# Seven products in one PSUM bank and another order of the steps, in a two-layer decoder trunk on one core

## The chip, the cores and the metric

One core of a Trainium2 chip runs the whole kernel. The metric is the device time of one execution in microseconds. TensorE (PE) multiplies, VectorE (DVE) and ScalarE (ACT) do the element work, GpSimd (POOL) and SyncE (SP) here only issue DMAs.

## The reference

Two layers; each is `x + mixed @ w_out`, with one input projection that feeds four groups of four heads. Cut to what matters:

```python
h = rms_norm(x, norm_g)                       # x: 256 x 2048
p = split_columns(h @ w_in)                   # q, k, v, gate of each group, and small ones
fox  = forgetting_attention(q, k, v, log_sigmoid(fox_f + fox_fb))
diff = rms_norm(softmax(q1 k1) v - lam * softmax(q2 k2) v)
moba = causal attention (256 keys are one block)
gla  = gated linear attention, in chunks of 64
mixed = concat([fox, diff, moba, gla], each times silu(its gate))
x = x + mixed @ w_out
```

After the second layer one more RMS norm. All inputs and the output are float32.

## The kernel before

**Weights.** Each weight tile is split into a high part (`hi`, written by ACT) and the rest (`lo`, written by DVE as weight minus high part), and so is the activation (`hTp` for the projections, `mTh` and `mTl` for the mixed groups in the output projection). A product is the sum of three: activation high by weight high, activation low by weight high, activation high by weight low. The weights stream in the order of use: SP loads them in steps of 512 KB, that is two 128 x 512 tiles, into five buffers (`raw`); `hi` and `lo` have four buffers, and are made three steps ahead of PE. A **block** is 512 columns of the projection in eight steps; a normal step is 12 matmuls with 512 columns, for two row tiles of 128 rows (`m` is 0 and 1) in one PSUM bank each. At a block's end ACT or DVE read the two banks (the evacuation).

**The seven products.** diff's and MoBA's values (`diff_v`, `moba_v`) are not projected in blocks but together, by Strassen's scheme: seven products p1 to p7 of sums of the quarters, four **form steps** of 6 matmuls each, 28 per layer. The sums of weights come by accumulating DMAs on POOL, those of activations from DVE. A form step uses up one 512 KB load in half the PE time of a normal step. Two PSUM banks take turns for the products.

**PSUM.** Eight banks of 128 x 512 float32: four for blocks and products (`mm0a`, `mm0b`, `mm1a`, `mm1b`), two pairs for everything else (`side`).

**What sets the order.** The program is written out step by step in a loop: `prepare(i + 3)` issues the hi part of a later step, then PE's matmuls of step `i`, then `tick()` gives out side work, then `complete(i + 3)` issues the lo part. Every engine takes its instructions in that order. Side work (rotary, softmax, gates, GLA, the norms) consists of generator tasks. `tick` keeps a small model of time: `times.now` moves with PE's matmuls, every DVE and ACT operation has a modelled end, and a task gets its next turn when its data is modelled to be there within LEAD (1.5 us). No more side work is given out while DVE's or ACT's modelled queue (`v_.tail`, `a_.tail`) reaches more than AHEAD past now. The side matmuls of a task stand in PE's queue at the place where the task was given its turn, so if the model was too hopeful, PE stands still there.

**Data that has to be transposed** goes through `turned`: a DVE stream transpose, four DMA writes on SP to a buffer in DRAM (`far`), and one DMA on POOL that reads it back. The model counts 4.5 us for the write, 6.5 for the read. The names in the profile: `four` and `eight` are working tiles of the side tasks; `fz` is FoX's forget gate, `an` GLA's small input, `fe` the exponentials that lead to `fz`.

**A task's PSUM.** `take_side` and `take_both` wait for a free pair of side banks.

The lines: L436 is the helper that issues nearly every matmul, L270 the helper of DVE and ACT operations, L276 that of DMAs through `far`, L1395 and L1359 the weight loads.

Of the kernel before, what the change touches and what calls it, by code (L numbers as in the profile page):

```python
# [21 lines left out]
P = 128  # L22
# [4 lines left out]
H = 4  # L27
# [82 lines left out]
def _blocks():  # L110
# [10 lines left out]
    for l in range(DEPTH):  # L121
        for cols in (
# [24 lines left out]
def _pair_steps(l):  # L147
# [3 lines left out]
    if not BY_DMA:  # L151
        raws.update({"p6": ("22",), "p4": ("21",)})
    return [{"pair": l, "form": f, "c": c, "from": [(q, c) for q in raws.get(f, ())], "first": c == 0, "last": c == 3}
            for f in ("p1", "p5", "p6", "p3", "p7", "p2", "p4") for c in range(4)]


NAMES = {13: "diff_v", 15: "moba_v"}


def _steps():  # L160
# [35 lines left out]
    for s in steps:  # L196
        if "pair" in s:
            s["at"] = {q: place((s["pair"], q), P * 1024) for q in s["from"] + [("12", s["c"])] * (s["form"] == "p1")}
# [5 lines left out]
def pair_part(q, c):  # L204
# [3 lines left out]
    return kts, COL[NAMES[PAIR[int(q[1]) - 1]]]  # L208
# [134 lines left out]
def hybrid_trunk(  # L343
# [52 lines left out]
    ranks = {"now": 0}  # L396
    ready = set()
    env = {}
    wakes = {}

    def tick(limited=True):
# [3 lines left out]
        for t in list(tasks):  # L405
            if max(v_.tail, a_.tail) > times.now + AHEAD:
                break
            for _ in range(3):
                if wakes[id(t)] > times.now + LEAD:
                    break  # L410
                times.latest, ranks["now"] = 0.0, ranks[id(t)]
                try:
                    next(t)
                except StopIteration:
                    tasks.remove(t)
                    del ranks[id(t)], wakes[id(t)]
# [1352 lines left out]
```

## Time and profile before

| | |
|---|---|
| median of 3 runs | 928.11 us (927.74 to 928.21) |
| the profiled execution's own time | 931.0 us |
| its span, first to last instruction | 928.9 us |
| mean granted TensorE clock | 0.986 |
| busy: PE, DVE, ACT | 893.5, 662.8, 563.7 us |
| data moved by DMA | 227.44 MB, 245 GB/s in the mean |

A row of the timeline or of a list of groups gives start and duration in us, engine, line, operation, output and inputs, and in square brackets how long the engine idled just before it and what ended that. A row of the waits gives what an engine waited for: us in all, how often, and the longest. Buffer numbers are left out of the profile's names.

### The profile page before, as it was taken

Reading aid. Unit: us, or ns where it says so; the run is one execution under the profiler, and the core shown is the slowest. Engines: PE = TensorE matmul, PEld = TensorE weight load, DVE = VectorE, ACT = ScalarE, POOL = GpSimd, SP = SyncE. Lnnn points to the kernel's source line nnn. Section 1 sums busy time; section 2 is a strip of 40 time slices with the busy share of each in tenths; the row PEclk is TensorE's granted clock in tenths of the full one; section 3 lists DMA queues with packets and bytes.
Section 4 is the critical chain, followed back from the end, with each engine's and each line's share of the span. In section 5 each row is a group of like instructions: output and inputs, shape, how many; then the busy total and the mean of one; then the engine's idle time right before and its main releaser. Section 6 shows DMA issues by size and latency. Waiting matters only on the chain.

```text
span 928.9 us, 12468 instructions
## 1 busy us (share of the span) xinstructions
PE 893.5 (96%) x4380; PEld 756.8 (81%) x4380; DVE 662.8 (71%) x943; ACT 563.7 (61%) x850; POOL 61.6 (7%) x87
## 2 busy tenths in 40 slices
PE   9989999999998999989999989999999989999996
PEld 7977789888786788878899868898878768788886
DVE  6679767688784884837668958777885849565783
ACT  6577665566654666735656965464863646575561
POOL 1001100001100000100000011000101000010100
PEclk9999999999998999999999999999999989999998
DMA  8769877648898477876878798676799763969952
GB/s 297 260 192 301 296 236 227 213 162 249 235 304 310 158 250 273 272 271 206 286 236 285 254 319 223 182 233 222 236 308 313 257 223 123 311 199 302 321 158 91
DMA packets 84141, 227.44 MB, mean 245 GB/s; under 512 B 9979, under 2 KB 30443, under 8 KB 83950
## 3 DMA queue, kind: packets, MB, share of 16 engines
q1 hardware_dynamic: 73336, 192.00, 60.6%
q0 software_dynamic: 9152, 33.03, 13.7%
q10 hardware_dynamic: 1590, 1.62, 0.6%
q8 instruction: 34, 0.56, 0.2%
q14 instruction: 29, 0.24, 0.1%
HBM read 204.06 MB, written 22.55 MB: 244 GB/s over the span
## 4 chain that ended last, share of the span: by engine, by line
PE 75%; DMA 11%; DVE 6%; issue 3%; ACT 3%; SPq 1%; POOL 0%; ACTq 0%; DVEq 0%; POOLq 0%
PE mm0a L436 16%; PE mm0b L436 15%; PE mm1b L436 15%; PE mm1a L436 15%; PE side L436 13%; DMA raw<-in_weights 6%; DMA far<-four 3%; DVE lo L270 3%; DMA four<-far 2%; DVE four L270 1%; ACT hi L270 1%; ACT four L270 1%; DMA four<-in_gla_wa 0%; DVE mx L270 0%; SPq L276 0%
## 5 line engine op out<-in xcount | busy, mean ns | idle before, releaser
L270 DVE TENSOR_TENSOR lo<-raw,hi 128x1024 fp32r<-128x1024 f32 (+2 forms) x319 | 363.6, 1156 | 126.8 <-ACT hi L270 118.9
L270 ACT ACTIVATE hi<-raw 128x1024 fp32r<-128x1024 f32 (+2 forms) x319 | 316.5, 1009 | 196.7 <-PE mm0b L436 52.1
L436 PE MATMUL mm0a<-hi,hTp 128*128 128x512 f32 (+1 forms) x448 | 168.3, 385 | 2.6 <-ACT hi L270 2.2
L436 PE MATMUL mm1a<-hi,hTp 128*128 128x512 f32 (+1 forms) x448 | 168.1, 384 | 2.4 <-ACT four L270 1.9
L436 PE MATMUL mm0b<-hi,hTp 128*128 128x512 f32 (+1 forms) x432 | 162.9, 382 | 0.1
L436 PE MATMUL mm1b<-hi,hTp 128*128 128x512 f32 (+1 forms) x432 | 162.6, 382 | 0.1
L436 PEld LDWEIGHTS mm0a<-hi,hTp 128*128 128x128 f32 x448 | 84.7, 189 | 19.7 <-ACT hi L270 3.8
L436 PEld LDWEIGHTS mm1a<-hi,hTp 128*128 128x128 f32 x448 | 84.6, 189 | 18.3 <-ACT four L270 2.3
L436 PEld LDWEIGHTS mm1b<-hi,hTp 128*128 128x128 f32 x432 | 81.7, 189 | 14.9 <-ACT four L270 0.8
L436 PEld LDWEIGHTS mm0b<-hi,hTp 128*128 128x128 f32 x432 | 81.9, 189 | 14.7 <-ACT four L270 0.6
L436 PE MATMUL mm0a<-lo,hTp 128*128 128x512 f32 (+1 forms) x224 | 84.3, 382 | 0.8 <-DVE lo L270 0.7
L436 PE MATMUL mm1a<-lo,hTp 128*128 128x512 f32 (+1 forms) x224 | 83.7, 380 | 0.4 <-DVE lo L270 0.4
L436 PE MATMUL mm0b<-lo,hTp 128*128 128x512 f32 (+1 forms) x216 | 81.2, 379 | 0.0
L436 PE MATMUL mm1b<-lo,hTp 128*128 128x512 f32 (+1 forms) x216 | 81.0, 379 | 0.0
L276 POOL DMA_DIRECT2D four<-far x40 | 22.1, 553 | 525.7 <-DMA far<-four 169.0
L436 PE MATMUL side<-four,four 128*128 128x128 f32 (+3 forms) x336 | 41.4, 302 | 12.1 <-DMA four<-far 6.6
L436 PEld LDWEIGHTS side<-four,four 128*128 128x128 f32 (+1 forms) x336 | 39.5, 208 | 15.7 <-DMA four<-far 7.4
L436 PEld LDWEIGHTS mm0a<-lo,hTp 128*128 128x128 f32 x224 | 42.4, 189 | 9.3 <-DVE lo L270 1.6
L436 PEld LDWEIGHTS mm1a<-lo,hTp 128*128 128x128 f32 x224 | 42.1, 188 | 8.3 <-DVE lo L270 0.8
L436 PEld LDWEIGHTS mm0b<-lo,hTp 128*128 128x128 f32 x216 | 40.8, 189 | 7.2
L436 PEld LDWEIGHTS mm1b<-lo,hTp 128*128 128x128 f32 x216 | 40.5, 188 | 7.2
L270 ACT ACTIVATE four<-four 128x512 fp32r<-128x512 f32 (+3 forms) x44 | 35.2, 821 | 17.1 <-DMA four<-far 14.1
(190 smaller groups left out, 1272.4 us busy)
## 6 DMA issues: line engine op xcount, KB each, us to landing
raw<-in_weights SPq DMA_DIRECT2D x271, 512.0 KB, 5.1
four<-far POOLq DMA_DIRECT2D x34, 512.0 KB, 6.4
far<-four SPq DMA_DIRECT2D x128, 128.0 KB, 4.9
raw<-in_weights SPq DMA_DIRECT2D x46, 348.0 KB, 4.4
xs<-in_weights POOLq DMA_DIRECT2D x24, 512.0 KB, 8.6
xs<-in_weights SPq DMA_DIRECT2D x8, 512.0 KB, 7.3
xs<-in_x SPq DMA_DIRECT2D x4, 512.0 KB, 10.4
kept<-xs SPq DMA_DIRECT2D x1, 2048.0 KB, 8.1
```

The costliest lines, as they stand in the source:

```text
L270: return f(*args, **kw)
L276: self.eng.dma_start(out, src, **kw)
L436: t_.matmul(out, lhsT, rhs, start=start, stop=stop, **kw)
```

## The change

- The form steps stand one by one: after steps 3, 6 and 8 of each block from the 3rd to the 11th, and one in the 12th. Before, two or three in a row stood behind each of these blocks.
- The order of the products is p2, p5, p3, p1, p6, p7, p4 where it was p1, p5, p6, p3, p7, p2, p4. diff's values are complete after 24 form steps (before 20), MoBA's after 28 (as before).
- All seven products use one PSUM bank. The other three banks of the four rotate among the blocks (`mm0` to `mm3`); before, the products held a pair and the blocks the other pair.
- In a block's first and last step the matmuls of row tile 0 all come ahead of those of row tile 1 (before they alternated), but for the first three steps of the program.
- The evacuation of a block is issued ahead of the next hi part, before behind it.
- The model: AHEAD 5.0 where it was 3.0; write 5.0 and readback 7.5 where they were 4.5 (3.0 in one place) and 6.5; a task that takes side banks waits until SAFE (1.0 us) past its data's modelled end, and times of data are handed from task to task (`given_out`, `until`).

The counts of instructions on PE, DVE, POOL and SP stay as they are; ACT has four table loads fewer. Two evacuations of products go from ACT to DVE and two from DVE to ACT.

```diff
@@ -37,19 +37,27 @@
...
-PAIR = (15, 13)
-FORMS_AFTER = {3: 3, 4: 3, 5: 3, 6: 2, 7: 3, 8: 3, 9: 3, 10: 3, 11: 3, 12: 2}
-WITHIN = {12: 2}
+MIDDLE = ("gla_v", "fox_q", "fox_k", "fox_v", "fox_g", "diff_q", "diff_k", "moba_q", "moba_k", "diff_g", "moba_g", "moba_v", "diff_v")
+NAMES = ("moba_v", "diff_v")
+PAIR = tuple(3 + MIDDLE.index(z) for z in NAMES)
+FORMS_AT = {i: (3, 6, 8) for i in range(3, 12)}
+FORMS_AT[12] = (3,)
+FORM_ORDER = ("p2", "p5", "p3", "p1", "p6", "p7", "p4")
...
-SUM_OF = {"p5": 3, "p6": 0, "p3": 1, "p7": 2}
+SUM_OF = {"p5": 3, "p3": 0, "p6": 1, "p7": 2}
...
-AHEAD = 3.0
+AHEAD = 5.0
...
+SAFE = 1.0
+ROOM = 5.0
+WRITE = 5.0
+READ = 7.5
@@ -151,10 +153,7 @@
...
-            for f in ("p1", "p5", "p6", "p3", "p7", "p2", "p4") for c in range(4)]
-NAMES = {13: "diff_v", 15: "moba_v"}
+            for f in FORM_ORDER for c in range(4)]
...
 def _steps():
@@ -175,14 +174,10 @@
...
-        for i, n in FORMS_AFTER.items():
+        for i, places in FORMS_AT.items():
...
-            within = WITHIN.get(i, 0)
-            if within:
-                at = own[len(own) // 2]
-                steps[at:at] = [rest.popleft() for _ in range(within)]
-            at = own[-1] + 1 + within
-            steps[at:at] = [rest.popleft() for _ in range(n - within)]
+            for z, at in enumerate(places):
+                steps.insert(own[0] + at + z, rest.popleft())
@@ -384,43 +379,50 @@
...
     def take_side():
+        yield SAFE
...
     def take_both():
+        yield SAFE
...
-    ranks = {"now": 0}
-    ready = set()
+    ranks = {"now": 0, "task": None, "room": AHEAD}
+    ready = {}
...
+    ends = {}
+    def given_out(key):
+        ready[key] = max(times.latest, ends.get(ranks["task"], 0.0))
...
     def tick(limited=True):
...
-            if max(v_.tail, a_.tail) > times.now + AHEAD:
+            if v_.tail > times.now + AHEAD or a_.tail > times.now + ranks["room"]:
...
-                times.latest, ranks["now"] = 0.0, ranks[id(t)]
+                times.latest, ranks["now"], ranks["task"] = 0.0, ranks[id(t)], id(t)
...
-                    next(t)
+                    more = next(t)
...
-                    del ranks[id(t)], wakes[id(t)]
+                    del ranks[id(t)], wakes[id(t)], ends[id(t)]
...
-                wakes[id(t)] = times.latest
-        ranks["now"] = 0
+                ends[id(t)] = max(ends[id(t)], times.latest)
+                wakes[id(t)] = ends[id(t)] + LEAD + more if more else times.latest
+        ranks["now"], ranks["task"], times.latest = 0, None, 0.0
...
     def begin(task, l, gi=None):
...
-        ranks[id(task)], wakes[id(task)] = rank, 0.0
+        ranks[id(task)], wakes[id(task)], ends[id(task)] = rank, times.latest, times.latest
@@ -428,6 +430,8 @@
     def until(key):
...
+        times.latest = max(times.latest, ready[key])
+        yield
...
     def matmul(out, lhsT, rhs, start, stop, tiles=1, **kw):
@@ -468,9 +472,9 @@
...
-            q_.move(d[:, :, i].rearrange("j c f -> c j f"), t[32 * i:32 * i + 32].rearrange("c (j f) -> c j f", j=4), 4.5)
-        yield
-        g_.move(t, d.rearrange("j c i f -> (j c) (i f)"), 6.5)
+            q_.move(d[:, :, i].rearrange("j c f -> c j f"), t[32 * i:32 * i + 32].rearrange("c (j f) -> c j f", j=4), WRITE)
+        yield
+        g_.move(t, d.rearrange("j c i f -> (j c) (i f)"), READ)
@@ -1555,33 +1561,30 @@
...
-        a, b = st["ps"]
-        for i, at in ((0, "p1"), (1, "p5")):
+        a = st["ps"]
+        for i, at in ((0, "p2"), (1, "p5")):
             if f == at:
...
-        r0 = r1 = env["r", l]
-        nr = env["r", l, -1.0]
-        if f == "p1":
-            a_.activation(st["t", 0][:, 0], a, AF.Copy, scale=r0[:, 0:1])
+        r, nr = env["r", l], env["r", l, -1.0]
+        left, right = st["t", 0], st.get(("t", 1))
+        if f == "p2":
+            a_.activation(left[:, 0], a, AF.Copy, scale=r[:, 0:1])
         elif f == "p5":
-            a_.activation(st["t", 1][:, 1], b, AF.Copy, scale=r1[:, 1:2])
+            a_.activation(right[:, 1], a, AF.Copy, scale=r[:, 1:2])
+        elif f == "p3":
+            a_.activation(right[:, 0], a, AF.Copy, scale=r[:, 0:1])
+        elif f == "p1":
+            v_.scalar_tensor_tensor(left[:, 0], a, r[:, 0:1], left[:, 0], op0=OP.mult, op1=OP.add)
         elif f == "p6":
-            a_.activation(st["t", 1][:, 0], a, AF.Copy, scale=nr[:, 0:1])
-        elif f == "p3":
-            t = st["t", 1][:, 0]
-            v_.scalar_tensor_tensor(t, b, r1[:, 0:1], t, op0=OP.mult, op1=OP.add)
+            v_.scalar_tensor_tensor(right[:, 0], a, nr[:, 0:1], right[:, 0], op0=OP.mult, op1=OP.add)
         elif f == "p7":
-            t = st["t", 1]
-            v_.scalar_tensor_tensor(t[:, 1], a, nr[:, 1:2], t[:, 1], op0=OP.mult, op1=OP.add)
-            given(l, PAIR[1], t)
-        elif f == "p2":
-            t = st["t", 0]
-            v_.scalar_tensor_tensor(t[:, 0], b, r0[:, 0:1], t[:, 0], op0=OP.mult, op1=OP.add)
+            v_.scalar_tensor_tensor(right[:, 1], a, nr[:, 1:2], right[:, 1], op0=OP.mult, op1=OP.add)
+            given(l, PAIR[1], right)
         elif f == "p4":
-            a_.activation(st["t", 0][:, 1], a, AF.Copy, scale=r0[:, 1:2])
-            given(l, PAIR[0], st["t", 0])
+            a_.activation(left[:, 1], a, AF.Copy, scale=r[:, 1:2])
+            given(l, PAIR[0], left)
...
     def given(l, i, t):
@@ -1610,10 +1613,12 @@
...
-        for x, part, j, kt in products:
-                for m in range(2):
-                    matmul(ps[m][:, :n], x[:, kt, m * P:(m + 1) * P], s[part][:, j],
-                           s["first"] and j == 0 and x is lh and part == "hi", part == "lo" and (True, j) == end)
+        products = [(*z, m) for z in products for m in range(2)]
+        if (s["first"] or s["last"]) and not any(s is z for z in plan[:HALVED]):
+            products.sort(key=lambda z: z[4])
+        for x, part, j, kt, m in products:
+            matmul(ps[m][:, :n], x[:, kt, m * P:(m + 1) * P], s[part][:, j],
+                   s["first"] and j == 0 and x is lh and part == "hi", part == "lo" and (True, j) == end)
...
     def results(b):
@@ -1648,26 +1653,30 @@
...
-    banks = {"n": 1, "s": None}
+    banks = {"next": deque(range(4)), "s": None}
...
     def settle(waiting, bank=None):
...
-                if bank is None or all(b["bank"] != bank for b in waiting):
+                if bank is None or all(bank not in b["banks"] for b in waiting):
...
+            times.latest = 0.0
...
-    def take_bank(k):
+    def take_bank(keep=True):
+        k = banks["next"].popleft()
+        if keep:
+            banks["next"].append(k)
...
-        return [mm.tile([P, 512], F32, name=f"mm{k}{m}", bufs=1) for m in "ab"]
+        return k, mm.tile([P, 512], F32, name=f"mm{k}", bufs=1)
@@ -1693,44 +1702,46 @@
...
+        if banks["s"] is not None and "done" in pairs[banks["s"]]:
+            banks["next"].append(pairs[banks["s"]]["bank"])
+            banks["s"] = None
+        settle(waiting)
         prepare(i + ahead)
...
-        if banks["s"] is not None and "done" in pairs[banks["s"]]:
-            banks["s"] = None
-        settle(waiting)
-        while not s["need"] <= ready:
+        while not s["need"] <= ready.keys():
...
-            if s["form"] == "p1" and s["first"]:
-                k = 1 - banks["n"]
-                pairs[s["pair"]] = {"bank": k, "ps": take_bank(k)}
+            if s["form"] == FORM_ORDER[0] and s["first"]:
+                k, ps = take_bank(False)
+                pairs[s["pair"]] = {"bank": k, "ps": ps}
...
-                ready.add(("paired", s["pair"], SUM_OF[s["form"]]))
+                given_out(("paired", s["pair"], SUM_OF[s["form"]]))
...
-                b["bank"] = None
+                b["banks"] = ()
...
-                    b["bank"] = banks["n"] = 1 - (banks["n"] if banks["s"] is None else pairs[banks["s"]]["bank"])
-                    b["ps"] = take_bank(b["bank"])
+                    b["banks"], b["ps"] = zip(*[take_bank() for _ in range(2)])
...
+        ranks["room"] = ROOM if s["last"] else AHEAD
...
+        ranks["room"] = AHEAD
```
Three places of the order, before and after. Numbers behind a name tell buffers' uses apart; `hi_N` and `lo_N` are one step's weight parts.

*The transpose of diff's second queries in layer 1, on DVE.* Before:

```order
L270 TENSOR_TENSOR lo_6325<-raw_6250,hi_6324 128x1024
L270 TENSOR_TENSOR mTl_114<-four1_6356,mTh_113 128x2x4x128
L270 STREAM_TRANSPOSE four11_6390<-four7_6228 128x1024
L270 TENSOR_TENSOR lo_6374<-raw_6262,hi_6373 128x1024
L270 TENSOR_TENSOR lo_6396<-raw_6283,hi_6395 128x1024
L270 TENSOR_TENSOR lo_6419<-raw_6301,hi_6418 128x1024
```

After:

```order
L265 TENSOR_TENSOR lo_6288<-raw_6211,hi_6287 128x1024
L265 TENSOR_TENSOR lo_6310<-raw_6230,hi_6309 128x1024
L265 STREAM_TRANSPOSE four0_6345<-four1_6284 128x1024
L265 TENSOR_TENSOR lo_6331<-raw_6245,hi_6330 128x1024
L265 TENSOR_TENSOR lo_6351<-raw_6264,hi_6350 128x1024
```

Before, the transpose stands ahead of the lo part of the fifth step before the scores; those five steps (12, 6, 6, 6 and 12 matmuls) are 42 matmuls, the end of the second and all of the third and fourth shown below. Now it is the sixth step, lo_6331, and the six (12, 12, 12, 6, 12, 12) are 66.

*The same scores on PE, with the steps ahead of them.* Before:

```order
L436 MATMUL mm0b_4813<-lo_6396,hTp_112 128x512 x2
L436 MATMUL mm0b_4813<-hi_6418,hTp_112 128x512 x4
L436 MATMUL mm0b_4813<-lo_6419,hTp_112 128x512 x2
L436 MATMUL mm0b_4813<-hi_6436,hTp_112 128x512 x4
L436 MATMUL mm0b_4813<-lo_6437,hTp_112 128x512 x2
L436 MATMUL mm1a_6508<-hi_6455,hTp_112 128x512
L436 MATMUL mm1b_6509<-hi_6455,hTp_112 128x512
```

Behind this step, whose matmuls go on alternating between the two banks, the scores follow (`side0_6524<-four11_6390`). After:

```order
L440 MATMUL mm2_6312<-hi_6424,hTp_112 128x512 x4
L440 MATMUL mm2_6312<-lo_6425,hTp_112 128x512 x2
L440 MATMUL mm3_6313<-hi_6424,hTp_112 128x512 x4
L440 MATMUL mm3_6313<-lo_6425,hTp_112 128x512 x2
L440 MATMUL side1_6491<-four0_6345,four3_6241 128x128 x8
L440 MATMUL mm1_4688<-hi_6443,mTh_113 128x512 x2
L440 MATMUL mm1_4688<-hi_6443,mTl_114 128x512 x2
L440 MATMUL mm1_4688<-lo_6444,mTh_113 128x512 x2
L440 MATMUL mm0_6540<-hi_6456,hTp_112 128x512 x4
```

Three form steps in a row (x4 and x2 into mm0b) became one (into mm1) between two blocks, and the last step of a block and the first of the next have their row tiles apart.

*The activations that lead to fz in layer 0, on ACT.* Before:

```order
L270 ACTIVATE hi_964<-raw_895 128x1024
L270 ACTIVATE fe_981<-fx_710 128x8
L270 ACT_TABLE_LOAD
L270 ACTIVATE fe_981<-fe_981 128x8
L270 ACT_TABLE_LOAD
L270 ACTIVATE fe_981<-fe_981 128x8
L270 ACTIVATE hi_990<-raw_916 128x1024
```

After:

```order
L265 ACTIVATE fe_824<-fx_701 128x8
L265 ACT_TABLE_LOAD
L265 ACTIVATE fe_824<-fe_824 128x8
L265 ACTIVATE hi_831<-raw_738 128x1024
L265 ACT_TABLE_LOAD
L265 ACTIVATE fe_824<-fe_824 128x8
L265 ACTIVATE hi_854<-raw_757 128x1024
```

The product with fz stood on PE behind the last matmul of lo_931, the step ahead of hi_943; now it stands behind that of lo_878, three steps behind hi_831. One hi part is now made between the activations.

More of the change, by code (lines that the diff above doesn't have):

```diff
@@ L197, in _steps @@
         if "pair" in s:
-            s["at"] = {q: place((s["pair"], q), P * 1024) for q in s["from"] + [("12", s["c"])] * (s["form"] == "p1")}
+            s["at"] = {q: place((s["pair"], q), P * 1024) for q in s["from"] + [("12", s["c"])] * (s["form"] == FORM_ORDER[0])}
         else:
@@ L564, in constants @@
         s2.put(w3)
-        ready.add("constants")
+        given_out("constants")
         yield
@@ L616, in split_x @@
         s4.put(t)
-        ready.add(("h", l, chunk))
+        given_out(("h", l, chunk))
     def make_hT(l, chunk, parts):
@@ L626, in make_hT @@
             square_sum(parts, m, c, chunk)
-        ready.add(("sq", l, chunk))
+        given_out(("sq", l, chunk))
         t, z = yield from joined(box)
@@ L649, in know_rows @@
         env["r", l] = r
-        ready.add(("r", l))
+        given_out(("r", l))
     def rows_of(l, ps, dst, func=AF.Copy, factor=1.0):
@@ L665, in split_group @@
         s4.put(t)
-        ready.add(("m", l, gi))
+        given_out(("m", l, gi))
     def gated_rows(o, ops, rs, sg):
@@ L742, in gla_turn @@
         env["gla_qk", l] = yield from put_in_order(s4, w, v)
-        ready.add(("gla_qk", l))
+        given_out(("gla_qk", l))
     def gla_gate(l, ps):
@@ L768, in given @@
             env[name, l] = t
-            ready.add((name, l))
+            given_out((name, l))
         return given
@@ L1069, in fox_forget @@
         env["forget", l] = z
-        ready.add(("forget", l))
+        given_out(("forget", l))
     def fox(l):
@@ L1106, in turn @@
                 env[name, l] = z, v
-            ready.add((name, l))
+            given_out((name, l))
         def given(l, t):
@@ L1129, in done @@
             env[name, l] = sg
-            ready.add((name, l))
+            given_out((name, l))
         return done
@@ L1265, in final_weights @@
         yield
-        ready.add("fng")
+        given_out("fng")
     def final_part(chunk, c):
@@ L1307, in final_rows @@
             nc.sync.dma_start(rows[:, q], xs[:, m, q])
+    middle = {
+        "gla_v": whole_rows(keeps("gla_v"), 0.125),
+        "fox_q": by_rows("fox_q"), "fox_k": by_rows("fox_k", fox), "fox_v": fox_v, "fox_g": gate_rows("fox_g", True),
+        "diff_q": by_rows("diff_q", None, "rope_d", DIFF_HALF, 64), "diff_k": by_rows("diff_k", diff, "rope_d", DIFF_HALF, 64),
+        "diff_v": whole_rows(keeps("diff_v")), "diff_g": gate_rows("diff_g", False),
+        "moba_q": by_rows("moba_q", None, "rope_m", MOBA_HALF, HD), "moba_k": by_rows("moba_k", moba, "rope_m", MOBA_HALF, HD),
+        "moba_v": whole_rows(keeps("moba_v")), "moba_g": gate_rows("moba_g", True),
+    }
     dones = []
@@ L1339, in hybrid_trunk @@
         if "pair" in s:
-            orders += [("y", i, None)] * (s["form"] == "p1") + [("raw", i, q) for q in s["from"]]
+            orders += [("y", i, None)] * (s["form"] == FORM_ORDER[0]) + [("raw", i, q) for q in s["from"]]
         else:
@@ L1416, in split_xt @@
         if kts[-1] % 4 == 3:
-            ready.add(("h", 0, kts[-1] // 4))
+            given_out(("h", 0, kts[-1] // 4))
     def first_rms():
@@ L1495, in sum_forms @@
         s4.put(z)
-        ready.add(("forms", l))
+        given_out(("forms", l))
     def keep_rows(l):
@@ L1502, in keep_rows @@
         nc.sync.dma_start(kept, xs.rearrange("p m d -> p (m d)"))
-        ready.add("kept")
+        given_out("kept")
     def sum_early(s):
@@ L1630, in prepare @@
             s = plan[i]
-            while s.get("here", 0) < (len(s["from"]) + (s["form"] == "p1") if "pair" in s else 1):
+            while s.get("here", 0) < (len(s["from"]) + (s["form"] == FORM_ORDER[0]) if "pair" in s else 1):
                 tick(False)
```

30 lines of the change are left out of this document (9 added, 21 removed).

## The prediction

> **What bounds the kernel now.** I read the page's busy times first, then the list of what TensorE (PE) waited for, then each of those waits on the timelines.
>
> ```profile
> span 928.9 us, 12468 instructions
> PE 893.5 (96%) x4380; PEld 756.8 (81%) x4380; DVE 662.8 (71%) x943; ACT 563.7 (61%) x850; POOL 61.6 (7%) x87
> ```
>
> PE is busy for 96% of the span, VectorE (DVE) for 71%, and the change leaves PE's matmuls as they are. So only what PE does not use can be won: 928.9 - 893.5 = 35.4 us. This list says where most of it lies (waited for, us in all, times, longest):
>
> ```profile
> PE side L436 <- DMA four<-far: 6.6, 2, 4.5
> PE side L436 <- ACT four L270: 2.9, 1, 2.9
> PE side L441 <- ACT an L270: 2.6, 2, 1.7
> PE side L436 <- DVE four L270: 2.6, 2, 2.1
> PE side L436 <- DVE fz L270: 2.3, 1, 2.3
> PE mm0a L436 <- ACT hi L270: 2.2, 2, 1.8
> PE mm0a L436 <- ACT mTh L270: 2.1, 1, 2.1
> PE mm1a L436 <- ACT four L270: 1.9, 1, 1.9
> PE mm0a L436 <- DVE lo L270: 1.1, 2, 0.7
> PE mm1a L436 <- DVE lo L270: 1.0, 2, 0.6
> PE side L531 <- PEq L1758: 0.8, 1, 0.8
> PE mm1a L436 <- ACT hi L270: 0.5, 1, 0.5
> PE mm0a L436 <- ACT four L270: 0.3, 1, 0.3
> PE mm1b L436 <- DVE lo L270: 0.3, 1, 0.3
> PE mm0a L436 <- DVE mTl L270: 0.3, 1, 0.3
> ```
>
> The rows add up to 27.5 us; the other 7.9 us lie mostly behind PE's last matmul, and I leave them as they are. The weight stream itself (hi and lo, the split weights) costs only 2.2 + 1.1 + 1.0 + 0.5 + 0.3 = 5.1 us. The rest is side work that is late: PE runs in order, so a side product whose data isn't there holds up every weight step behind it.
>
> A wait costs more than its idle time where the granted clock drops behind it. The stretches around six waits (us, PE busy and instructions, the other engines, PEclk, DMA share, GB/s):
>
> ```profile
> 292.00:300.00 8.00, 6.39 (x36) 5.82 (x36) 3.64 (x5) 3.07 (x5) 0.00 (x0) 0.57 0.66 264
> 404.00:412.00 8.00, 5.65 (x17) 3.92 (x16) 6.02 (x7) 7.73 (x9) 0.00 (x0) 0.79 0.50 171
> 543.00:551.00 8.00, 4.17 (x15) 2.26 (x14) 4.45 (x12) 7.60 (x15) 1.31 (x2) 1.00 1.06 276
> 746.00:754.00 8.00, 5.92 (x26) 4.93 (x27) 3.72 (x5) 1.00 (x6) 0.00 (x0) 0.57 0.21 86
> 98.00:106.00 8.00, 5.68 (x21) 4.33 (x20) 5.90 (x12) 7.30 (x11) 0.00 (x0) 0.79 0.83 313
> 801.00:809.00 8.00, 5.95 (x30) 4.76 (x29) 1.56 (x4) 4.09 (x5) 1.07 (x2) 1.00 1.01 365
> ```
>
> Two stretches lose 0.43 x 8 = 3.4 us of clock, two 0.21 x 8 = 1.7 us. Taking off the part in which PE idled anyway, I count 3.0 us at 292, 2.6 at 746, 1.6 each at 98 and 404: 8.8 us. So 27.5 + 8.8 = 36.3 us can be won at most.
>
> The largest wait, by its own rows on PE:
>
> ```profile
> 742.92 0.39 PE L436 MATMUL mm1a<-lo,hTp 128*128 128x512 f32 x1
> 743.15 0.39 PE L436 MATMUL mm1b<-lo,hTp 128*128 128x512 f32 x1
> 748.08 2.08 PE L436 MATMUL side<-four,four 64*128 64x128 f32 x16 [4.55 <-DMA four<-far]
> ...
> 751.11 0.63 PE L436 MATMUL mm1a<-hi,hTp 128*128 128x512 f32 x1
> 751.54 0.63 PE L436 MATMUL mm1b<-hi,hTp 128*128 128x512 f32 x1
> ```
>
> A 128x512 matmul follows the last after 0.23 us at the full clock, after 0.43 behind this wait. A normal weight step (12 of them) is thus 2.7 us, a step of the seven products (6 of them, a form step) 1.36 us. The data came by this chain, on DVE, SP and POOL:
>
> ```profile
> 730.67 1.24 DVE L270 STREAM_TRANSPOSE four<-four 128x1024 f32<-128x1024 f32 x1
> ```
> ```profile
> 733.46 1.91 SPq L276 DMA_DIRECT2D far<-four  x4
> ```
> ```profile
> 739.61 0.56 POOL L276 DMA_DIRECT2D four<-far  x1 [33.29 <-DVE four L270]
> ```
>
> The transpose ended at 731.9 and the scores began at 748.08: 16.2 us for write and readback, for which the order's model allows 4.5 + 6.5 = 11 us.
>
> **The change part by part.** (1) *Side products later.* The model now allows 5.0 + 7.5 + 1.0 (SAFE) = 13.5 us. The order shows what this does for diff's scores of layer 1: behind the transpose stand the lo parts of 42 of PE's 512-wide matmuls that precede the scores, and now of 66. That is 24 x 0.227 = 5.4 us more, against a wait of 4.55: it goes, with its 2.6 us of clock. MoBA's scores (2.05, at 806) have their write three weight steps earlier. Of 6.6 + 2.6 = 9.2 us I let 0.8 stay: **-8.4** (bounds 0 and -9.2).
>
> (2) *fz, an, mTh.* fz stood directly ahead of its product; its three activations now stand among earlier hi parts, and the product follows fz by about 24 matmuls, 5.4 us, against 2.3 us of wait: of 2.3 + 1.6 I keep 0.5, **-3.4**. For an, the order sets 9.2 us of PE's work where 5.4 stood, against two waits of 2.6 us together: **-2.0**. The side work that ends in diff's mTh begins some 48 us of PE's work ahead of the first step that needs it, not 38, against 2.1 + 0.3 + 1.6 = 4.0 us: **-3.5**. Together -8.9 (bounds 0 and -10.5).
>
> (3) *FoX's second product*, 2.9 + 0.5 idle and 3.0 clock in layer 0, 2.1 in layer 1: 8.5 us. Here two causes mix. On SP the far writes stood in one heap:
>
> ```profile
> 270.36 4.83 SPq L276 DMA_DIRECT2D far<-four  x8
> 275.29 0.38 SPq L1395 DMA_DIRECT2D raw<-in_weights  x1
> 275.71 1.95 SPq L276 DMA_DIRECT2D far<-four  x4
> 277.76 0.94 SPq L1395 DMA_DIRECT2D raw<-in_weights  x2
> 278.75 3.34 SPq L276 DMA_DIRECT2D far<-four  x4
> 282.19 6.58 SPq L1395 DMA_DIRECT2D raw<-in_weights  x4
> ```
>
> Sixteen writes take 4.83 + 1.95 + 3.34 = 10.1 us of SP's queue with three weight loads among them, and four more wait behind; the new order sets 7 or 8 loads among as many. But in layer 0 the last activation and the last sums still stand directly ahead of the product on ACT and DVE, so I keep 4.0: **-4.5** (bounds 0 and -8.5).
>
> (4) *One form step at a time, and one bank.* Three form steps in a row use up three 512 KB loads in 4.1 us, where
>
> ```profile
> raw<-in_weights SPq DMA_DIRECT2D x271, 512.0 KB, 5.1
> four<-far POOLq DMA_DIRECT2D x34, 512.0 KB, 6.4
> far<-four SPq DMA_DIRECT2D x128, 128.0 KB, 4.9
> ```
>
> one load takes 5.1 us to land (several are in flight). At 545 such a trio met an ACT queue whose head stood on a readback:
>
> ```profile
> 543.40 1.06 ACT L270 ACTIVATE four<-four 128x1024 f32<-128x1024 f32 x1 [7.86 <-DMA four<-far]
> ```
>
> Behind it waited a hi part (1.8 us of PE) and a bank's results (1.9). Single form steps give ACT two normal steps, 5.4 us, to catch up, and the plan allows a readback 1 us more before its user is given out; of 3.7 I keep 2.0: **-1.7** (0 to -3.7). The small waits for lo, hi and results (27.5 less all named, and less PEq's 0.8: about 3.6) lose **0.8** (0 to -2). The single product bank must be empty before the next product starts; at least two normal steps lie between, 5.4 us for one evacuation. A block's first bank has been free for a block's length; its second is the first of the block before, whose products now end 1.36 us before that block does, with a form step between (1.36) and 1.36 us until it is written: 4.1 us, as much as the three form steps gave. I cost both at nothing; if ACT were 5 us late, each of 12 changes of product would cost up to 1 us.
>
> (5) *Row tiles apart at a block's ends.* The first lo is needed after 4 matmuls, not 8: 0.9 us earlier, in some 80 of 340 steps, where PE waits for lo at 5 places now. Between 0 and 80 x 0.9 = 72 us if every lo came at the last moment, which 5 waits in 340 exclude; I take **+2.0**. (6) *AHEAD 5.0.* Up to 2 us more side work may stand ahead of a hi or lo: **+1.0** (bounds 0 and +24, the slower rival). ACT's four fewer table loads and the exchanged evacuations lie off the path.
>
> Sum: -8.4 - 8.9 - 4.5 - 1.7 - 0.8 + 3.0 = **-21.3 us**. The profiled execution took 931.0 us, its span 928.9; 931.0 - 21.3 = 909.7. The median run before was 928.11, 2.9 below the profiled one. Whether that difference is stalls of the same kind I can't see, so I take off a little over half of it: **908 us**.
>
> A rule weighed: the Trainium skill (TensorE: Matmul & The Clock Gate, Part 1: The HAM clock gate) has the clock halve after an idle window of about 3.4 us. Here a 2.32 us wait at 100 was followed by the low clock and a 2.05 us one at 806 was not, so the trace sets the limit lower. By the page, the clock terms at 98 and 404 (3.2 us) would not hang on these waits and would stay, and the sum would be -18.1, 911 us; the rows decide for me.
>
> **The rivals.** *A. The DMA engines keep the stalls* (914 to 921). No transfer is taken out, only moved. The DMA share is 1.06 and 1.01 in the stretches at 543 and 801, and the readback at 739.61 needed 8.4 us against 6.4 in the median. If three quarters of (1), (3) and 545 stay, that is 0.75 x (9.2 + 8.5 + 3.7) = 16.1 us, 9.3 more than the 6.8 I keep: -12.0 in all, 919 beside the profiled run, 917 in the median. Against it: at 746 the share is 0.21, so the wait there was a late start. The Trainium skill (Trainium Kernel Development and Optimization, Key Constraints) says that DMAs of SP, ACT and POOL share the same 16 engines, whichever queue issues them; that speaks for A.
>
> *B. Slower: side work in front of hi and lo* (930 to 935). With AHEAD 5.0 instead of 3.0, DVE and ACT may hold 2 us more side work when a weight part is issued, and the part's step follows 3 steps later. Where the part's margin is under 2 us, PE waits the difference. The gains of 24.3 us are used up from about 24 steps at 1 us, 7% of 340; at 30 steps it is 933. For: DVE is 71% busy and more than that near the attention stages. Against: 8 waits for hi and lo in 340 steps now, and single form steps loosen the tightest places.
>
> *C. The stalls move* (926 to 930): diff's v comes at form step 24 instead of 20 and MoBA's at 28, so later side work is pressed against the projections' end, and what was won in the middle is lost at the second product of diff and MoBA. That needs some 20 us at two places per layer, 5 us each: more than the longest wait now.
>
> *D. Nearly every wait goes* (894 to 899): -36.3 + 3 = -33.
>
> **How the numbers follow.** Forecast 0.57 (900 to 915), A 0.22, D 0.07, C 0.05, B 0.09. A measurement of this kernel tells about 0.2% (2 us) from no change. Faster: 0.57 + 0.22 + 0.07 + a little of C = 0.87; within 0.2%: 0.04; slower: 0.09. The range holds the forecast and A and cuts B, C and half of D: 897 to 922.
>
> **What would show it.** The waits for DMA four<-far, fz, an and mTh should be gone or under 1 us each, idle PE near 17 us, the granted clock low in at most one stretch before the end; FoX's product in layer 0 should still be the longest wait, 2 to 4 us. If the sum of waits for lo and hi grows beyond 8 us, (5) and (6) were priced too low; if raw or four<-far are named for over 8 us, A holds. If DVE's and ACT's busy time differ by more than some 6 us, something moved that I did not see.

## The result and the profile after

The changed kernel takes **901.57 us** (median of 4 runs, 900.71 to 902.47), the kernel before 928.16 us beside it: a ratio of 0.9712, 95% interval 0.9695 to 0.9729. The forecast was 908 us, range 897 to 922. The direction and the range held; the gain is 26.6 us where 20 were forecast. The time lies at the lower end of the forecast's 900 to 915 us, close to rival D.

The profiled execution took 902.47 us, its span is 900.7 us. In the changed kernel the helpers stand at L440 (matmuls), L265 (DVE and ACT) and L271 (DMAs through `far`), the weight loads at L1402 and L1366. Busy times of the engines, then everything that PE waited for (us in all, times, longest):

```profile
PE 884.1 (98%) x4380; PEld 751.8 (83%) x4380; DVE 662.3 (74%) x943; ACT 560.5 (62%) x846; POOL 61.7 (7%) x87
```
```profile
PE mm L440 <- DVE lo L265: 3.0, 4, 1.4
PE mm L440 <- ACT four L265: 3.0, 2, 2.3
PE mm L440 <- ACT hi L265: 2.2, 1, 2.2
PE side L535 <- PEq L1769: 0.8, 1, 0.8
```

Fifteen rows became four, and 27.5 us of waits 9.0. PE idles for 900.7 - 884.1 = 16.6 us, where it was 35.4, and its busy time fell by 9.4 us with the same 4380 matmuls, most of it because the clock is now low only once before the end (0.996 in the mean, 0.986 before). DVE and ACT do the same work (0.5 and 3.2 us less), so this is a gain in order alone.

No wait of a side tile on moved or side data is left. Diff's scores of layer 1, which stood for 4.55 us, on PE; and the transpose, the write and the readback that feed them, on DVE, SP and POOL:

```profile
722.27 0.94 PE L440 MATMUL side<-four,four 64*128 64x128 f32 x12
```
```profile
701.61 1.24 DVE L265 STREAM_TRANSPOSE four<-four 128x1024 f32<-128x1024 f32 x1
```
```profile
704.36 2.35 SPq L271 DMA_DIRECT2D far<-four  x4
```
```profile
711.15 0.56 POOL L271 DMA_DIRECT2D four<-far  x1 [2.74 <-DMA far<-four]
```

From the transpose's end, 702.85, to the scores are 19.4 us, where the chain before needed 16.2: no idle time stands in brackets behind the scores.

What is left lies at three places in the main: near 61, near 88 (1.43 us for a lo part) and near 533. The first and the last on PE:

```profile
61.00 2.00 PE L440 MATMUL mm<-hi,hTp 128*128 128x512 f32 x4 [2.22 <-ACT hi L265]
...
533.41 1.21 PE L440 MATMUL mm<-hi,hTp 128*128 128x512 f32 x4 [2.28 <-ACT four L265]
```

At 61 PE now waits for a hi part. On ACT the small activations that make `an`, and those of the first block's gate, stand ahead of it; the first of them waits 1.51 us for `rstd`, which POOL computes beside its DMAs (at 57.24).

```profile
57.55 1.28 ACT L265 ACT_TABLE_LOAD   x1
58.84 0.54 ACT L265 ACTIVATE four<-mm,rstd 128x332 f32<-128x332 f32 x1
59.28 0.29 ACT L265 ACTIVATE an<-mm,rstd 128x48 f32<-128x48 f32 x1
59.88 1.06 ACT L265 ACTIVATE hi<-raw 128x1024 fp32r<-128x1024 f32 x1
```

They stood ahead of it before the change too, as ACT's rows show; there PE's next instruction was the product with `an`, and it waited for `an` itself (the last row, PE):

```profile
57.97 0.29 ACT L270 ACTIVATE an<-mm0b,rstd 128x48 f32<-128x48 f32 x1
58.15 0.54 ACT L270 ACTIVATE four<-mm0b,rstd 128x332 f32<-128x332 f32 x1
58.57 1.07 ACT L270 ACTIVATE hi<-raw 128x1024 fp32r<-128x1024 f32 x1
```
```profile
58.31 0.33 PE L441 MATMUL side<-ct,an 128*128 128x128 f32 x1 [1.72 <-ACT an L270]
```

So here one wait took the place of another, behind the same row of work.

The last is the place that stalled at 549 before. ACT's hi parts wait there for weight loads, and a block's evacuation stands behind them and 2.44 us of side work:

```profile
528.02 1.06 ACT L265 ACTIVATE hi<-raw 128x1024 fp32r<-128x1024 f32 x1 [2.25 <-DMA raw<-in_weights]
528.99 2.44 ACT L265 ACTIVATE four<-ct,dgs 128x128 f32<-128x128 f32 x8
531.73 1.06 ACT L265 ACTIVATE hi<-raw 128x1024 fp32r<-128x1024 f32 x1 [0.30 <-DMA raw<-in_weights]
532.69 1.25 ACT L265 ACTIVATE four<-mm,r0.125_4134 128x512 f32<-128x512 f32 x2
```

### The profile page after: what moved, and what is told of

Read it like the earlier page. It is cut to its first block, busy times and chain, and to the rows that moved or that the text cites. A ratio compares the mean times of both kernels' runs of the same rounds, so it can differ in the third digit from the quotient of the medians.

```text
span 900.7 us, 12457 instructions
## 1 busy us (share of the span) xinstructions
PE 884.1 (98%) x4380; PEld 751.8 (83%) x4380; DVE 662.3 (74%) x943; ACT 560.5 (62%) x846; POOL 61.7 (7%) x87
## 2 busy tenths in 40 slices
DMA packets 84141, 227.44 MB, mean 253 GB/s; under 512 B 9979, under 2 KB 30443, under 8 KB 83950
## 4 chain that ended last, share of the span: by engine, by line
PE 88%; ACT 4%; DMA 3%; DVE 2%; issue 2%; SPq 0%; POOL 0%; POOLq 0%; DVEq 0%; ACTq 0%
PE mm L440 75%; PE side L440 13%; DMA raw<-in_weights 2%; ACT hi L265 1%; ACT L265 1%; DVE lo L265 1%; ACT four L265 1%; DVE four L265 1%; DVE tq L265 0%; DMA four<-in_xt 0%; DMA gng<-in_gla_norm_gt 0%; SPq L271 0%; ACT eight L265 0%; ACT mTh L265 0%; ACT fe L265 0%
## 5 line engine op out<-in xcount | busy, mean ns | idle before, releaser
L265 ACT ACTIVATE hi<-raw 128x1024 fp32r<-128x1024 f32 (+2 forms) x319 | 317.3, 1010 | 203.8 <-PE mm L440 118.0
L440 PE MATMUL mm<-hi,hTp 128*128 128x512 f32 (+1 forms) x1760 | 432.4, 382 | 5.3 <-ACT four L265 3.0
L265 DVE TENSOR_TENSOR lo<-raw,hi 128x1024 fp32r<-128x1024 f32 (+2 forms) x319 | 362.7, 1155 | 98.3 <-ACT hi L265 91.9
L440 PEld LDWEIGHTS mm<-hi,hTp 128*128 128x128 f32 x1760 | 323.3, 189 | 66.1 <-ACT hi L265 4.0
L440 PE MATMUL mm<-lo,hTp 128*128 128x512 f32 (+1 forms) x880 | 238.5, 381 | 3.0 <-DVE lo L265 3.0
L440 PEld LDWEIGHTS mm<-lo,hTp 128*128 128x128 f32 x880 | 162.4, 188 | 35.2 <-DVE lo L265 5.8
L440 PE MATMUL mm<-hi,mTh 128*128 128x512 f32 (+1 forms) x256 | 69.7, 379 | 0.0
L440 PE MATMUL mm<-hi,mTl 128*128 128x512 f32 (+1 forms) x256 | 69.0, 376 | 0.0
L440 PE MATMUL mm<-lo,mTh 128*128 128x512 f32 (+1 forms) x256 | 69.0, 376 | 0.0
L440 PEld LDWEIGHTS mm<-hi,mTl 128*128 128x128 f32 x256 | 46.3, 188 | 8.9
L440 PEld LDWEIGHTS mm<-lo,mTh 128*128 128x128 f32 x256 | 46.3, 188 | 8.9
L271 POOL DMA_DIRECT2D four<-far x40 | 21.9, 547 | 450.2 <-DVE lo L265 183.9
L440 PEld LDWEIGHTS mm<-hi,mTh 128*128 128x128 f32 x256 | 45.7, 188 | 8.0
L265 ACT ACTIVATE four<-mm,rstd 128x512 f32<-128x512 f32 (+2 forms) x56 | 36.6, 667 | 24.7 <-PE mm L440 24.4
L265 ACT ACTIVATE four<-four 128x512 fp32r<-128x512 f32 (+3 forms) x44 | 35.1, 816 | 16.6 <-DMA four<-far 12.1
L265 DVE STREAM_TRANSPOSE four<-four 128x1024 f32<-128x1024 f32 (+1 forms) x34 | 38.6, 1140 | 1.8 <-ACT four L265 1.8
L440 PEld LDWEIGHTS side<-four,four 128*128 128x128 f32 (+1 forms) x336 | 36.3, 190 | 2.5 <-issue 1.4
L440 PE MATMUL side<-four,four 128*128 128x128 f32 (+3 forms) x336 | 37.3, 281 | 0.0
L265 DVE TENSOR_TENSOR four<-four,four 128x512 fp32r<-128x512 f32 (+3 forms) x31 | 26.7, 883 | 9.2 <-ACT four L265 9.2
L271 POOL DMA_DIRECT2D xs<-in_weights x24 | 21.1, 879 | 177.3 <-DVE lo L265 60.2
L265 ACT ACTIVATE hi<-xs 128x1024 fp32r<-128x1024 f32 x24 | 25.4, 1058 | 8.7 <-PE mm L440 8.6
L265 DVE TENSOR_TENSOR lo<-xs,hi 128x1024 fp32r<-128x1024 f32 x24 | 29.1, 1214 | 0.5 <-ACT hi L265 0.4
```

The costliest lines, as they stand in the source:

```text
L265: return f(*args, **kw)
L271: self.eng.dma_start(out, src, **kw)
L440: t_.matmul(out, lhsT, rhs, start=start, stop=stop, **kw)
```

## The experiments

Ratios are to the kernel before on the same chip, with 95% intervals. On the chips of these runs that kernel had medians of 927 to 930 us and single times from 922 to 938, so the ratio is what is compared. One execution of each kernel was profiled, and the waits are those of that execution.

### The allowances undone

```diff
-SAFE = 1.0
+SAFE = 0.0
-WRITE = 5.0
-READ = 7.5
+WRITE = 4.5
+READ = 6.5
```

> The changed kernel with the old allowances: SAFE 0.0 where it is 1.0, WRITE 4.5 for 5.0, READ 6.5 for 7.5; steps, banks and AHEAD stay. Theory M (the side products given out later took the waits away): the order sets five side products directly behind their ACT or DVE producers again (FoX, MoBA and diff, in both layers), so waits on the side tiles come back, for DMA four<-far and for ACT or DVE four; half of the 26.6 us or more is lost, 914 to 922 us. Theory S (the single form steps and the three rotating banks did it): waits for side tiles stay under 4 us in all, 901 to 906 us.

934.37 us, ratio 1.0054 (1.0012 to 1.0095): the whole gain is gone, more than theory M had. But the mechanism isn't the one that it named. PE's waits in this kernel, the largest:

```profile
PE mm L440 <- ACT four L265: 8.4, 4, 2.9
PE side L440 <- ACT four L265: 5.9, 3, 2.5
PE mm L440 <- DVE lo L265: 5.9, 8, 2.4
PE mm L440 <- ACT hi L265: 4.9, 4, 1.9
PE side L440 <- DMA four<-far: 2.9, 1, 2.9
```

PE itself waits for a readback only once, 2.9 us. Of the 19.2 us that it waits for ACT (banks, side tiles and hi), 16.1 us, in eight waits, end within 2.1 us of the end of a wait of ACT on a readback: all four for banks, all three for side tiles and one for hi. ACT's waits on readbacks, in this kernel, in the change, and before:

```profile
ACT four L265 <- DMA four<-far: 65.0, 18, 6.5
```
```profile
ACT four L265 <- DMA four<-far: 19.8, 9, 4.3
```
```profile
ACT four L270 <- DMA four<-far: 36.2, 9, 9.7
```

And one such place, on ACT with the old allowances: 6.48 us of waiting, then the two evacuations of a block, then the next hi.

```profile
322.23 1.06 ACT L265 ACTIVATE four<-four 128x1024 f32<-128x1024 f32 x1 [6.48 <-DMA four<-far]
323.19 1.25 ACT L265 ACTIVATE four<-mm,rstd 128x512 f32<-128x512 f32 x2
324.33 1.05 ACT L265 ACTIVATE hi<-raw 128x1024 fp32r<-128x1024 f32 x1
```

So the allowances are worth here what they take off the front of ACT's queue. The sum of ACT's waits alone doesn't give the time, though: what counts is what stands behind them (see AHEAD 4.0).

### SAFE alone undone

```diff
-SAFE = 1.0
+SAFE = 0.0
```

> The changed kernel with SAFE 0.0 alone; write and readback stay at 5.0 and 7.5. If the wait of 1 us before a task takes its side banks carries the gain, the ACT queue's waits for DMA four<-far rise from 20 us to 50 or more, as with all three old numbers (65 us), and it takes 920 to 932 us. If the two allowances carry it, the waits stay near 20 to 30 us and it takes 903 to 912 us.

906.91 us, 0.9766 (0.9714 to 0.9818). The 1 us before side banks isn't what carries the gain; its effect, 0 to 1%, can't be told from the change itself, and ACT's wait on readbacks is 23.6 us, near the change's 19.8. It takes the write and readback allowances, alone or together with SAFE, to lose the gain; the two without SAFE were not run.

### AHEAD

```diff
-AHEAD = 5.0
+AHEAD = 3.0
-ROOM = 5.0
+ROOM = 3.0
```

> The changed kernel with AHEAD and ROOM 3.0 as before, not 5.0. If AHEAD 5.0 is what gives the order its room (side work early enough), some side waits come back and it takes 905 to 912 us. If AHEAD 5.0 only puts side work in front of hi and lo, as step (6) of the prediction had it (+1.0 us, with a slower rival behind it), the waits for ACT hi and DVE lo (5.2 us in all now) shrink to 2 to 4 us and it takes 897 to 901 us.

928.45 us, 0.9988 (0.9958 to 1.0019): again the whole gain, where I had expected it to be a little faster. Two waits make most of it, one at the end of each layer (the rest is lower clock, 0.987 in the mean against 0.996, and 3.6 us more of other waits); this is PE in layer 0:

```profile
PE mm L440 <- ACT mTh L265: 17.2, 2, 9.0
```
```profile
406.17 2.08 PE L440 MATMUL mm<-hi,mTh 128*128 128x512 f32 x4 [8.21 <-ACT mTh L265]
```

With less room, side work runs late through the layer (FoX's second product stands at 243.85, in the change at 226.46), and at its end the last group isn't mixed when the output projection needs it. ACT and SP at that place:

```profile
402.55 1.06 ACT L265 ACTIVATE hi<-raw 128x1024 fp32r<-128x1024 f32 x1 [7.12 <-DMA raw<-in_weights]
403.52 1.13 ACT L265 ACTIVATE four<-four,dng 128x1024 f32<-128x1024 f32 x1
405.07 1.04 ACT L265 ACTIVATE mTh<-four 128x1024 fp32r<-128x1024 f32 x1
```
```profile
388.30 7.10 SPq L271 DMA_DIRECT2D far<-four  x12
395.50 0.38 SPq L1402 DMA_DIRECT2D raw<-in_weights  x1
```

The late side work also heaps its far writes, twelve in a row, ahead of a weight load; ACT's hi waits 7.12 us for that load, and the mixing stands behind the hi. Two sizes between and beyond:

```diff
-AHEAD = 5.0
+AHEAD = 4.0
-ROOM = 5.0
+ROOM = 4.0
```

> The changed kernel with AHEAD and ROOM 4.0. Theory R: no product stands directly behind mTh in the order any more, so most of the 27 us between AHEAD 3.0 and 5.0 is back: 900 to 910 us, with no wait for mTh above 2 us. Rival L (the change's numbers fit together by luck, and any other number breaks the order): 915 us and more, with waits at places that are new.

911.07 us, 0.9799 (0.9751 to 0.9847). The wait for mTh is gone and two thirds of the gain are there; 12.1 us of waits for lo, hi and banks remain, against 8.2. That is 1 us outside theory R's range and under that of rival L: the order doesn't break, but it doesn't get all of the gain either.

```diff
-AHEAD = 5.0
+AHEAD = 6.0
-ROOM = 5.0
+ROOM = 6.0
```

> The changed kernel with AHEAD and ROOM 6.0. Theory R: the room was enough at 5.0; the same within 1%, 898 to 908 us. The price of AHEAD by step (6) of the prediction, more side work in front of hi and lo: waits for hi and lo 2 us above those of the change, 903 to 908 us. Rival L: 915 us and more.

914.14 us, 0.9849 (0.9785 to 0.9912): slower than at 5.0. Here the price that the prediction put on AHEAD shows, on ACT more than on DVE:

```profile
PE mm L440 <- ACT four L265: 7.5, 3, 4.1
PE mm L440 <- ACT hi L265: 7.1, 4, 3.1
PE mm L440 <- DVE lo L265: 2.8, 3, 1.6
```

The profiled execution was this kernel's longest, 921.0 us; the other three took 912 to 915. ACT's waits on readbacks are 34.5, 41.4, 19.8 and 47.4 us for AHEAD 3.0, 4.0, 5.0 and 6.0: they don't follow the room, and with 41.4 us at AHEAD 4.0 the kernel still takes 911 us. Why 5.0 has so few isn't shown.

```diff
-ROOM = 5.0
+ROOM = 3.0
```

> The changed kernel with ROOM 3.0 alone: after a block's last step ACT is given side work only up to 3.0 us ahead, so that the evacuation stands nearer its front. If ACT's side work at a block's end makes the waits for a bank (ACT four, 3.0 us) and for hi (2.2 us), these fall under 2 us in all: 896 to 901 us. If the order reacts as to AHEAD 4.0 and 6.0, waits come up elsewhere: 905 to 915 us.

908.55 us, 0.9787 (0.9736 to 0.9838). It was meant to beat the change and doesn't: the waits for a bank are 4.5 us and those for lo 6.2, at other places. The order reacted as it did to the other sizes.

### The row tiles

```diff
-        if (s["first"] or s["last"]) and not any(s is z for z in plan[:HALVED]):
-            products.sort(key=lambda z: z[4])
```

> The changed kernel with the two row tiles alternating in the first and last steps again. The prediction had +2.0 us for the tiles apart, from a lo that is needed 0.9 us earlier; by that it takes 899 to 901 us and the wait for lo falls under 2 us. The rival: the tiles apart free a bank 1.36 us earlier, and without that the first matmul of a block waits for ACT four, 0.5 us at each of some 18 boundaries or more: 906 to 915 us.

907.12 us, 0.9745 (0.9685 to 0.9805). Inconclusive in size: the interval holds the change's 0.9712. It is not the 2 us faster that the prediction had as its middle. The waits for lo fall to 1.5 us, as expected, but those for banks rise from 3.0 to 4.8:

```profile
PE mm L440 <- ACT four L265: 4.8, 4, 2.5
PE mm L440 <- DVE lo L265: 1.5, 3, 0.8
```

### The form steps in threes and fours

```diff
-FORMS_AT = {i: (3, 6, 8) for i in range(3, 12)}
-FORMS_AT[12] = (3,)
+FORMS_AT = {i: (8, 8, 8) for i in range(3, 12)}
+FORMS_AT[12] = (8,)
```

> The changed kernel with three form steps in a row behind each block again (one behind the 12th), same product order and one bank. Theory S: a product ends within such a trio, so the next product waits for the bank to be emptied, about 1 us at 9 of 12 changes of product, and weight loads, lo and hi run late as before: waits for ACT hi, DVE lo and raw of 8 us and more, 912 to 922 us. Theory M: the side waits stay away (none for DMA four<-far), only the bank costs some 5 to 9 us: 906 to 911 us.

952.76 us, 1.0238 (1.0164 to 1.0312): slower than before the change by more than any theory said. The three largest waits:

```profile
PE mm L440 <- DVE four L265: 13.9, 4, 4.7
PE mm L440 <- DVE lo L265: 11.4, 6, 2.9
PE mm L440 <- ACT hi L265: 5.9, 3, 2.4
```

The first row is the one bank: a product that ends within a trio must be read by DVE before the next may start, up to 4.7 us. The read itself takes 0.74 us there; it stood on DVE behind a lo part that had waited 1.97 us for its hi (at 231.34). The next two are weights that come too late. To tell these apart, fours, which never change the product within a group:

```diff
-FORMS_AT = {i: (3, 6, 8) for i in range(3, 12)}
-FORMS_AT[12] = (3,)
+FORMS_AT = {i: (8, 8, 8, 8) for i in (3, 4, 6, 7, 8, 10, 11)}
```

> The changed kernel with the four form steps of each product together behind seven of the blocks, so that no product changes within such a group. If the one bank caused the 50 us of the run with threes, the waits for DVE four at a product's start (13.9 us there) go and so does most of the rest: 905 to 918 us. If form steps in a row are the cause themselves (four 512 KB loads, four hi and lo in 5.4 us), the waits for hi and lo stay at 17 us or more and the order stays bad: 930 to 950 us. In this order mTh stands directly ahead of its product at two places, which may add some 10 us either way and shows as its own wait.

946.56 us, 1.0189 (1.0127 to 1.0251). The waits (this kernel is a line shorter, so the helpers have other numbers):

```profile
PE mm L439 <- ACT mTh L264: 19.7, 2, 10.1
PE mm L439 <- DVE lo L264: 14.4, 7, 5.0
PE mm L439 <- ACT hi L264: 8.1, 5, 2.2
```

The bank's wait is gone, lo and hi rose to 22.5 us, and mTh to 19.7. So the bank alone isn't what makes such groups slow: form steps in a row are a cause by themselves. How much the bank cost in the threes can't be told, since the two ratios' intervals overlap and 19.7 us here are another wait. That the layer's late end comes from its upset middle is my reading and isn't shown.

### Parts of the change in the kernel before

```diff
-AHEAD = 3.0
+AHEAD = 5.0
```

> The kernel before with only AHEAD 5.0. Theory R: room without later allowances; side work stands earlier, some of the waits go, but ACT and PE still meet readbacks that the model has too early (ACT waits for DMA four<-far 36 us or more), 920 to 930 us. If AHEAD is the main gain by itself: 905 to 915 us. If it sets side work in front of hi and lo (the slower rival of the prediction): 932 us and more, with waits for hi and lo above 10 us.

955.78 us, 1.0282 (1.0233 to 1.0332). AHEAD alone does harm: PE waits 13.8 us for mTh at two places and ACT 50.2 us for readbacks. PE's waits for hi and lo are 12.6 us, so the slower rival's sign is there too.

```diff
-            q_.move(d[:, :, i].rearrange("j c f -> c j f"), t[32 * i:32 * i + 32].rearrange("c (j f) -> c j f", j=4), 4.5)
+            q_.move(d[:, :, i].rearrange("j c f -> c j f"), t[32 * i:32 * i + 32].rearrange("c (j f) -> c j f", j=4), 5.0)
-        g_.move(t, d.rearrange("j c i f -> (j c) (i f)"), 6.5)
+        g_.move(t, d.rearrange("j c i f -> (j c) (i f)"), 7.5)
...
```

> The kernel before with only the allowances for moved data changed: write 5.0, readback 7.5 (without SAFE, AHEAD 3.0). Theory M: the waits for DMA four<-far (6.6 us) go and it gains, 915 to 924 us. Theory R (later side work needs room at the layers' ends, which only AHEAD 5.0 gives): the order sets mTh directly ahead of its product at three or four places where before it was one, so the waits for mTh grow to 10 us and more and it is slower, 930 to 942 us.

936.17 us, 1.0079 (1.0048 to 1.011). ACT's waits for readbacks halve, from 36.2 to 18.9 us, but PE's own don't go (6.8 us, 6.6 before, now mostly in layer 0), so theory M fails. The side work is late at the end of layer 0, as theory R had it:

```profile
PE mm0a L436 <- ACT mTh L270: 12.0, 1, 12.0
PE side L436 <- DMA four<-far: 6.8, 3, 4.1
```

The same edit takes FoX's gate rows from 3.0 and 6.5 to 5.0 and 7.5. With both edits in the kernel before:

```diff
-AHEAD = 3.0
+AHEAD = 5.0
...
-            q_.move(d[:, :, i].rearrange("j c f -> c j f"), t[32 * i:32 * i + 32].rearrange("c (j f) -> c j f", j=4), 4.5)
+            q_.move(d[:, :, i].rearrange("j c f -> c j f"), t[32 * i:32 * i + 32].rearrange("c (j f) -> c j f", j=4), 5.0)
...
```

> The kernel before (its steps, banks and products) with three of the new numbers: AHEAD 5.0, write 5.0, readback 7.5, without SAFE. Alone AHEAD 5.0 made it 2.8% slower and the two allowances 0.8%. Theory C (room and allowances belong together, each alone only moves the waits): the ACT queue's waits for DMA four<-far fall from 50 us under 30, mTh stands directly ahead of its product at one place instead of two, and it takes 910 to 925 us. Theory S (without single form steps and the rotating banks no numbers help): 930 us and more, with waits for hi, lo and the banks above 10 us.

929.41 us, 1.0022 (0.9981 to 1.0064): no difference from before. The two repair each other's harm, as theory C had it (ACT's waits for readbacks 19.6 us, mTh 1.5), but PE still waits 12.3 us for hi, lo and banks, and 5.1 for an, which the change doesn't. So theory C is half right: they belong together; but without the rest of the change they bring nothing, and the time lies outside both ranges. The rest is the single form steps, the banks, the row tiles, the earlier evacuation, SAFE and the handing on of times; this run doesn't tell them apart.

## Why the prediction was right, and where not

**The reading of what can be won held.** 36.3 us of waits and lost clock were counted before. PE was to idle near 17 us, and it idles 16.6; that this came so near is in part luck. The prediction's own sum gives some 20 us (35.4 less 21.3, plus at least 5.8 that were clock and not idling), and the terms below were off in both directions. The stalls were a matter of order, not of transfers: with the same 227.44 MB, every wait of PE on moved data went. Rival A (the DMA engines keep the stalls) is out, but for the place at 533, where weight loads stand at the head of the chain and the DMA share is 1.02. The sentence of the Trainium skill (Trainium Kernel Development and Optimization, Key Constraints) on the shared DMA engines spoke for A; no run here speaks against the sentence, only the stalls weren't of that kind. Rival B wasn't met at AHEAD 5.0. Its waits came at 6.0 (9.9 us for hi and lo against 5.2) and in the kernel before with AHEAD 5.0 alone (12.6 us).

**(1) Side products later**, -8.4: both waits for four<-far and the low clock behind them are gone, -9.2. The size was right; the reason was half of it. That diff's data now has time enough is shown by the 19.4 us. But in the kernel before the longer allowances alone left PE 6.8 us of such waits, at other places. And undoing write, readback and SAFE cost 3.4% by the two ratios, some 32 us and not 8.4, of which only 2.9 us are PE's own wait for a readback. The step that failed is the place of that price: I had priced the allowances at PE's side products and left out that ACT takes work on readbacks too, with hi parts and evacuations behind it. I had seen that row (7.86 us on ACT at 543) and put it under the form steps.

**(2) fz, an, mTh**, -8.9: all three are gone, 10.5 us with their clock. But for an, -2.0, nothing was won: PE waits 2.2 us for the hi part behind the same activations, where it waited 2.6 for an, and the low clock behind it costs some 1.7 us (ten matmuls in 3.99 us where ten at 0.227 take 2.27). The step that failed is to take the product with an as the only one that this row of ACT's work holds up. So (2) gave some 6.6 us.

**(3) FoX's second product**, -4.5: this failed on the safe side. It was to stay the longest wait, 2 to 4 us; all 8.5 us went. The step that failed is the reading of the order: producers that stand directly ahead of a product on ACT and DVE don't make it wait if their engine has reached them in time. In layer 0 the last sums now end on DVE at 222.31, 4.1 us ahead of the product on PE:

```profile
221.02 1.29 DVE L265 TENSOR_TENSOR four<-four,four 128x512 fp32r<-128x512 f32 x2
```
```profile
226.46 2.48 PE L440 MATMUL side<-four,four 128*128 128x256 f32 x20
```

In the kernel before they came late because the hi part ahead of them on ACT waited for a weight load that was issued behind the heap of far writes; in layer 1 it was a weight load too (2.74 us, at 719.88).

```profile
290.83 1.06 ACT L270 ACTIVATE hi<-raw 128x1024 fp32r<-128x1024 f32 x1 [2.35 <-DMA raw<-in_weights]
```

**(4) Single form steps**, -1.7, with 0.8 of small waits: at 533 PE still waits 2.28 us for the bank at the same place of the program; the wait for hi went. The small waits for lo and banks didn't shrink (3.7 us, near 3.6). As a term of the sum it was nearly right, as a part of the change it was far too small: in threes the kernel takes 952.8 us. Beside the other edits I took the steps' place as a detail; but in none of the three kernels that had AHEAD 5.0 and the longer allowances with form steps in a row (929, 953 and 947 us) did the gain come.

**(5) and (6)**, together +3.0. For (5) the sign isn't shown: row tiles apart cost lo some 1.5 us and give banks 1.8, and the two ratios can't be told apart. (6) was wrong in sign within the changed kernel, and far off in size: AHEAD 5.0 was priced as side work in the way of hi and lo; its effect is that a layer's side work ends in time, and with 3.0 the kernel loses all it won (2.8% by the ratios, some 26 us). What it costs shows one step later, at 6.0.

So the sum of -21.3 became -28.5 in the profiled execution (931.0 to 902.47). Towards more, (3) makes 4.0 us, (5) and (6) 3.0 if they are counted as nothing, (1) 0.8, and the clock some 2: PE's busy time fell by 9.4 us with 1.7 of new low clock in it, where 8.8 were counted. Towards less, (2) makes 2.3 and (4) some 1. That the total came within 7 us is helped by this. Of the 1.7 us for the median against the profiled run, 0.9 is what the profiled run of the change lies above its own median; the one before lay 2.9 above.

**What stays open.** Four small steps away from the change's set of numbers (AHEAD with ROOM at 4.0 or 6.0, ROOM 3.0, SAFE 0.0) gave 907 to 914 us, ratios of 0.977 to 0.985. These four neighbours are 1.5 to 2.3% faster than before, the change 2.9%; so some 0.5 to 1.4% may belong to this one order, in which few things happen to collide (the change itself was not timed beside these runs, and SAFE 0.0 can't be told from it). Whether another set would do better was not tried beyond these. Also, single form steps with two banks were not tried, nor, each by itself, the new order of the products, the earlier evacuation and the handing on of times from task to task.

## What to carry to other kernels

In a schedule that a planner writes out in program order, a wrong estimate for a transfer can cost most on an engine that has other users behind it, as ACT did here: look at what ACT or DVE stand on with the weight parts queued behind, not only at what PE waits for. Room to work ahead and honest transfer times act together; each alone moved the stall to the end of the layer here, or in front of the weights. Before pricing one number of such a planner at nothing, undo it by itself, and expect its neighbours to differ by a per cent, as they did here, in ways that no single wait explains.

## What the hardware showed that was not expected

A wait of 2.22 us on PE was followed by the low clock at 61 (four matmuls in 1.8 us, 0.45 each), and one of 2.28 us at 533 was not (0.26 each). By the Trainium skill (TensorE: Matmul & The Clock Gate, Part 1: The HAM clock gate), whose idle window is about 3.4 us, neither should be; the trace differs at 61, and the measurement decides. So near 2.3 us the length of the idle time alone doesn't say whether the clock drops; before the change it was 2.32 with and 2.05 without. At the place near 61 other runs show both: 2.18 us with it (ROOM 3.0, four matmuls of this size in 1.74 us) and 2.19 without (form steps in threes, PEclk 1.00 from 56 to 64). The windows around both (PEclk is the third value from the end of a row):

```profile
56.00:64.00 8.00, 5.78 (x25) 4.90 (x24) 3.87 (x11) 6.74 (x11) 1.75 (x2) 0.82 0.92 250
...
529.00:537.00 8.00, 5.66 (x24) 3.90 (x23) 5.49 (x12) 7.67 (x15) 1.41 (x2) 1.00 1.02 395
```
